# Part of a row-maximum kernel's work moved from VectorE to GpSimd, with TensorE turning the data there and back

## The chip, the core and the metric

The kernel runs on one core of one Trainium2 chip. The metric is the device time of one execution in microseconds (us). Executions are sorted into fast and slow by their time and by the clock in their records, and experiments are compared with runs of the kernel before that were made on the same chip in the same rounds. "Span" is the profiled time from the first to the last instruction; it is about 2 us shorter than the device time.

## The reference

The input has 32 x 512 rows of 1024 numbers in fp32; the output is the maximum of each row.

```python
"x": np.random.randn(32, 512, 1024).astype(np.float32)
return np.max(x, axis=-1).astype(np.float32)
```

These are 16,384 rows. With one row on each of 128 partitions, they make 128 groups of 128 x 1024 elements. Such a group is called a *block* below: 0.52 MB, of 67.1 MB in all.

## The kernel before

Each load brings several blocks into a ring in SBUF (`ring` in the profile), and one VectorE instruction reduces all of them along the free dimension. The list of load sizes starts large and ends small, so that little is left to reduce once the last load has landed (one block here, 1.2 us).

```python
BLOCKS = [
    [15, 14, 13],
    [11, 9, 8, 7],
    [6, 6, 5, 4, 4, 4, 3, 2],
    [2, 2, 2, 2, 2, 1, 1, 1, 1, 1, 1, 1],
]
RING = 46
...
            xc = ring[:, at:at + g, :]
            nc.sync.dma_start(out=xc, in_=xb[:, b:b + g, :])
            nc.vector.reduce_max(out=res[:, first + b:first + b + g], in_=xc, axis=X)
...
        nc.scalar.dma_start(out=dst, in_=res[:, first:first + S])
```

Of the kernel before, what the change touches and what calls it, by code (L numbers as in the profile page):

```python
# [1 line left out]

# [4 lines left out]


F32 = mybir.dt.float32



BLOCKS = [
    [15, 14, 13],
    [11, 9, 8, 7],
    [6, 6, 5, 4, 4, 4, 3, 2],
    [2, 2, 2, 2, 2, 1, 1, 1, 1, 1, 1, 1],
]
RING = 46


@with_exitstack
def kernel(
    ctx: ExitStack,
    tc: tile.TileContext,
    x: bass.AP,
    out: bass.AP,
):
    nc = tc.nc
    P = 128  # L30
    X = mybir.AxisListType.X

    xf = x.flatten_outer_dims()
    N, D = xf.shape
    I = N // P
    of = out.flatten_outer_dims()

    once = ctx.enter_context(tc.tile_pool(name="once", bufs=1))
    ring = once.tile([P, RING, D], F32)
    res = once.tile([P, I], F32)  # L40

    at = first = 0
    for loads in BLOCKS:
        S = sum(loads)
        xb = xf[first * P:(first + S) * P, :].rearrange("(p i) d -> p i d", p=P)
        b = 0
        for g in loads:
            if at + g > RING:
                at = 0
            xc = ring[:, at:at + g, :]  # L50
            nc.sync.dma_start(out=xc, in_=xb[:, b:b + g, :])  # L51
            nc.vector.reduce_max(out=res[:, first + b:first + b + g], in_=xc, axis=X)  # L52
            at += g
            b += g
        dst = bass.AP(tensor=of.tensor, offset=of.offset + first * P, ap=[[S, P], [1, S]])
        nc.scalar.dma_start(out=dst, in_=res[:, first:first + S])
        first += S
    assert first == I


# [1 line left out]
_INS = ['x']  # L62
_OUTS = [((32, 512), 'float32')]


# [23 lines left out]
```

## Time and profile before

| | kernel before |
|---|---|
| device time, median of 3 runs | 165.6 us (165.55 to 165.71) |
| span | 163.6 us |
| VectorE busy | 138.4 us, 27 instructions |
| VectorE idle, waiting for a load | 22.8 us, of which 21.4 before the first |
| end of the last reduction | 161.25 us |
| last load complete on all 16 DMA engines (trace) | 159.6 us |

Busy time plus idle time gives the end of VectorE: 138.4 + 22.8 = 161.2 us. The lines behind the table are in the prediction.

### The profile page before, as it was taken

The page shows a single profiled execution, that of the slowest core. Times are in us where ns is not written, and L with a number is a line of the kernel's source. Part 1 is how long each engine was busy: PE and PEld are TensorE (multiplying, and loading weights), DVE is VectorE, ACT ScalarE, POOL GpSimd, SP SyncE. Part 2 cuts the span into 40 slices and gives each one's busy share as a digit, 9 for nine tenths or more (in the row PEclk, how much of TensorE's full clock was granted, in tenths as well). Part 3 has the DMA queues.
Part 4 walks back from the last instruction along what each step waited for, and adds up shares of the span by engine and source line. Part 5 has one row for each costly group of instructions (what it writes and reads, how often), then busy time and mean ns, then how long its engine had stood idle before and what let it go on. Part 6 is the DMA issues. An engine that isn't in the chain of part 4 may idle for free.

```text
span 163.6 us, 114 instructions
## 1 busy us (share of the span) xinstructions
DVE 138.4 (85%) x27; POOL 0.2 (0%) x4
## 2 busy tenths in 40 slices
DVE  0000079998999899999999999999999999999994
POOL 0000000000000000000000000000000000000000
DMA  7999699999999989999989999999999999999980
GB/s 240 481 481 436 285 449 449 449 449 417 417 417 417 529 353 529 388 425 401 459 385 465 449 401 427 439 400 459 419 421 421 445 405 421 421 421 415 409 339 2
DMA packets 4464, 67.18 MB, mean 411 GB/s; under 512 B 1008, under 2 KB 1008, under 8 KB 1904
## 3 DMA queue, kind: packets, MB, share of 16 engines
q1 hardware_dynamic: 3888, 67.11, 96.3%
q10 hardware_dynamic: 576, 0.07, 0.3%
HBM read 67.11 MB, written 0.07 MB: 411 GB/s over the span
## 4 chain that ended last, share of the span: by engine, by line
DVE 74%; DMA 23%; DVEq 1%; another core or an unknown queue 0%; SPq 0%; issue 0%
DVE res L52 74%; DMA ring<-in_x_dram 23%; DVEq L84 1%; SPq L51 0%
## 5 line engine op out<-in xcount | busy, mean ns | idle before, releaser
L52 DVE TENSOR_REDUCE res<-ring 128x1 f32<-128x1024 f32 (+12 forms) x27 | 138.4, 5205 | 22.8 <-DMA ring<-in_x_dram 22.8
L73 POOL MEMSET const-bfloat16-1.0<- 128x1 bf16 x1 | 0.1, 102 | 0.0
L73 POOL MEMSET const-uint8-127<- 128x1 uint8 x1 | 0.1, 102 | 0.0
L73 POOL MEMSET const-float32-0.0<- 128x1 f32 x1 | 0.1, 99 | 0.2 <-issue 0.2
L73 POOL MEMSET const-float32-1.0<- 128x1 f32 x1 | 0.1, 99 | 0.0
## 6 DMA issues: line engine op xcount, KB each, us to landing
ring<-in_x_dram SPq DMA_DIRECT2D x1, 7680.0 KB, 20.6
ring<-in_x_dram SPq DMA_DIRECT2D x1, 7168.0 KB, 37.2
ring<-in_x_dram SPq DMA_DIRECT2D x1, 6656.0 KB, 52.4
ring<-in_x_dram SPq DMA_DIRECT2D x2, 3072.0 KB, 33.3
ring<-in_x_dram SPq DMA_DIRECT2D x3, 2048.0 KB, 33.8
ring<-in_x_dram SPq DMA_DIRECT2D x6, 1024.0 KB, 23.9
ring<-in_x_dram SPq DMA_DIRECT2D x1, 5632.0 KB, 29.8
ring<-in_x_dram SPq DMA_DIRECT2D x1, 4608.0 KB, 24.9
```

The lines of the kernel that those rows point to most:

```text
L52: nc.vector.reduce_max(out=res[:, first + b:first + b + g], in_=xc, axis=X)
L73: nc = _bacc.Bacc("TRN2", target_bir_lowering=False, num_devices=1)
L84: with _tile.TileContext(nc) as tc:
```

## The change

Its intent is to relieve VectorE. From each of the first nine loads, one or two blocks are kept from it. TensorE turns (transposes) such a block in eight pieces of 128x128, by a product with an identity matrix; ScalarE copies the result from PSUM (`ps` in the profile) to SBUF (`sb`); GpSimd takes the maximum over partitions (an all-reduce); TensorE turns the resulting row back in eight pieces, and VectorE merges eight values a row. That is 14 of 128 blocks, about one row in seven of the large loads. The ring shrinks from 46 to 42 blocks, and the load sizes change.

```diff
 BLOCKS = [
-    [15, 14, 13],
-    [11, 9, 8, 7],
-    [6, 6, 5, 4, 4, 4, 3, 2],
-    [2, 2, 2, 2, 2, 1, 1, 1, 1, 1, 1, 1],
+    [(14, 2), (14, 2), (14, 2)],
+    [(14, 2), (13, 2), (9, 1)],
+    [(7, 1), (8, 1), (6, 1), (5, 0), (3, 0), (3, 0), (2, 0)],
+    [(2, 0), (2, 0), (2, 0), (2, 0), (1, 0), ... eight of these ...],
 ]
-RING = 46
+RING = 42
...
+    make_identity(nc, ident)
...
+        back = psmall.tile([P, m, C], F32)
+        for k in range(m):
+            ps = psum.tile([P, D], F32)
+            for c in range(C):
+                nc.tensor.transpose(out=ps[:, c * P:(c + 1) * P],
+                    in_=rows[:, k, c * P:(c + 1) * P], identity=ident)
...
+            nc.scalar.copy(out=sb, in_=ps)
...
+            nc.gpsimd.partition_all_reduce(top, sb, P, bass_isa.ReduceOp.max)
+            run(backs)
+            ... turn_back, put off in `backs`: eight transposes of top[0:1, ...] into back ...
+        return lambda: nc.vector.reduce_max(out=cols, in_=back, axis=X)
...
+            nc.vector.reduce_max(out=cols[:, :n - m], in_=xc[:, :n - m, :], axis=X)
+            run(late)              # the merge of the load before
+            if m:
+                late.append(merge)
```

More of the change, by code (lines that the diff above doesn't have):

```diff
@@ L6 @@
 from concourse._compat import with_exitstack
+from concourse import bass_isa
+from concourse.masks import make_identity
 F32 = mybir.dt.float32
 BLOCKS = [
-    [15, 14, 13],
-    [11, 9, 8, 7],
-    [6, 6, 5, 4, 4, 4, 3, 2],
-    [2, 2, 2, 2, 2, 1, 1, 1, 1, 1, 1, 1],
+    [(14, 2), (14, 2), (14, 2)],
+    [(14, 2), (13, 2), (9, 1)],
+    [(7, 1), (8, 1), (6, 1), (5, 0), (3, 0), (3, 0), (2, 0)],
+    [(2, 0), (2, 0), (2, 0), (2, 0), (1, 0), (1, 0), (1, 0), (1, 0), (1, 0), (1, 0), (1, 0), (1, 0)],
 ]
-RING = 46
+RING = 42
 @with_exitstack
@@ L34 @@
     N, D = xf.shape
+    C = D // P
     I = N // P
@@ L38 @@
     once = ctx.enter_context(tc.tile_pool(name="once", bufs=1))
+    turn = ctx.enter_context(tc.tile_pool(name="turn", bufs=2))
+    allr = ctx.enter_context(tc.tile_pool(name="allr", bufs=2))
+    psum = ctx.enter_context(tc.tile_pool(name="psum", bufs=3, space=bass.MemoryType.PSUM))
+    psmall = ctx.enter_context(tc.tile_pool(name="psmall", bufs=2, space=bass.MemoryType.PSUM))
     ring = once.tile([P, RING, D], F32)
     res = once.tile([P, I], F32)
+    ident = once.tile([P, P], F32)
+    make_identity(nc, ident)
@@ new lines, with by_gpsimd, turn_back @@
+    backs = []
+    late = []
+    def by_gpsimd(rows, cols, m):
+        back = psmall.tile([P, m, C], F32)
+        for k in range(m):
+            ps = psum.tile([P, D], F32)
+            for c in range(C):
+                nc.tensor.transpose(
+                    out=ps[:, c * P:(c + 1) * P],
+                    in_=rows[:, k, c * P:(c + 1) * P],
+                    identity=ident,
+                )
+            sb = turn.tile([P, D], F32)
+            nc.scalar.copy(out=sb, in_=ps)
+            top = allr.tile([P, D], F32)
+            nc.gpsimd.partition_all_reduce(top, sb, P, bass_isa.ReduceOp.max)
+            run(backs)
+            def turn_back(top=top, k=k):
+                for c in range(C):
+                    nc.tensor.transpose(
+                        out=back[:, k, c:c + 1],
+                        in_=top[0:1, c * P:(c + 1) * P],
+                        identity=ident[0:1, 0:1],
+                    )
+            backs.append(turn_back)
+        return lambda: nc.vector.reduce_max(out=cols, in_=back, axis=X)
@@ L42, with run @@
+    def run(calls):
+        while calls:
+            calls.pop(0)()
     at = first = 0
     for loads in BLOCKS:
-        S = sum(loads)
+        S = sum(n for n, m in loads)
         xb = xf[first * P:(first + S) * P, :].rearrange("(p i) d -> p i d", p=P)
         b = 0
-        for g in loads:
-            if at + g > RING:
+        for n, m in loads:
+            if at + n > RING:
                 at = 0
-            xc = ring[:, at:at + g, :]
-            nc.sync.dma_start(out=xc, in_=xb[:, b:b + g, :])
-            nc.vector.reduce_max(out=res[:, first + b:first + b + g], in_=xc, axis=X)
-            at += g
-            b += g
@@ L55 @@
-        dst = bass.AP(tensor=of.tensor, offset=of.offset + first * P, ap=[[S, P], [1, S]])
-        nc.scalar.dma_start(out=dst, in_=res[:, first:first + S])
+            xc = ring[:, at:at + n, :]
+            nc.sync.dma_start(out=xc, in_=xb[:, b:b + n, :])
+            cols = res[:, first + b:first + b + n]
+            if m:
+                merge = by_gpsimd(xc[:, n - m:, :], cols[:, n - m:], m)
+            else:
+                run(backs)
+            nc.vector.reduce_max(out=cols[:, :n - m], in_=xc[:, :n - m, :], axis=X)
@@ L57, with store @@
+            run(late)
+            if m:
+                late.append(merge)
+            at += n
+            b += n
+        def store(first=first, S=S):
+            dst = bass.AP(tensor=of.tensor, offset=of.offset + first * P, ap=[[S, P], [1, S]])
+            nc.scalar.dma_start(out=dst, in_=res[:, first:first + S])
+        late.append(store)
         first += S
+    run(late)
     assert first == I
```

## The prediction

Its sum came to this: outside the all-reduces 4.6 us a group, an estimate for the transposes, the copy, the turns back, the hand-overs, the merge (0.17 us, estimated from the 0.15 us an instruction and 1.066 us a block of the trace before); nine groups 41.4; the last merge at 20.2 + 112.0 + 41.4 = 173.6; the end of VectorE at 173.6 + 33.3 = 206.9; and with the tail and the offset 211 us, stated as 210.

> **What bounds the kernel now.** I read the page from the top: the busy times, the 40 slices, the DMA queues, the chain that ended last. Then I asked for the groups by shape, and for stretches of the span.
>
> ```profile
> span 163.6 us, 114 instructions
> DVE 138.4 (85%) x27; POOL 0.2 (0%) x4
> DVE  0000079998999899999999999999999999999994
> DMA  7999699999999989999989999999999999999980
> q1 hardware_dynamic: 3888, 67.11, 96.3%
> DVE 74%; DMA 23%; DVEq 1%; another core or an unknown queue 0%; SPq 0%; issue 0%
> ```
>
> VectorE (DVE) is busy for 85% of the span, and the load queue holds the 16 DMA engines for 96.3%: two resources close to full. GpSimd (POOL) does nothing, and TensorE and ScalarE have no row. The chain names VectorE for 74%, but it only follows the engine that finished last; it does not say that a faster VectorE would end sooner. For that I compare the two rates.
>
> ```profile
> L52 DVE TENSOR_REDUCE res<-ring 128x15 f32<-128x15360 f32 x1 | 16.2, 16153 | 21.4 <-DMA ring<-in_x_dram 21.4
> L52 DVE TENSOR_REDUCE res<-ring 128x14 f32<-128x14336 f32 x1 | 15.1, 15087 | 0.8 <-DMA ring<-in_x_dram 0.8
> L52 DVE TENSOR_REDUCE res<-ring 128x13 f32<-128x13312 f32 x1 | 14.0, 14020 | 0.6 <-DMA ring<-in_x_dram 0.6
> L52 DVE TENSOR_REDUCE res<-ring 128x2 f32<-128x2048 f32 x6 | 13.2, 2282 | 0.0
> ...
> L52 DVE TENSOR_REDUCE res<-ring 128x1 f32<-128x1024 f32 x7 | 8.0, 1216 | 0.0
> ```
>
> I call 1024 columns of all 128 partitions a block; there are 128 blocks. Two blocks take 2282 ns and one 1216, so VectorE needs 1.066 us a block and 0.15 us an instruction. The third load started VectorE at 54.06 us and the second at 38.33 (the chain in order of time), so 13 blocks came in 15.73 us: 1.21 us a block. **Transfers are the slower of the two.** All 128 blocks cost 128 x 1.21 = 154.9 us plus some 3 us to start. VectorE catches up with them through ever smaller loads:
>
> ```profile
> 158.00:160.00 2.00, 2.00 (x2) 0.00 (x0) 1.00 0.42 168
> 160.00:162.00 2.00, 1.25 (x2) 0.00 (x0) 1.00 0.00 0
> 162.00:164.00 2.00, 0.00 (x0) 0.00 (x0) 1.00 0.05 4
> ```
>
> The columns are the stretch, its length, VectorE busy, POOL busy, clock, DMA share, GB/s. Loads fill 0.42 of the stretch from 158 on, so their bytes end near 158.8 us. The last reduction starts at 160.0 and ends at 161.25. At most 1.2 us of VectorE backlog can be taken away; the rest of the end is one reduction and a store of 2.35 us. That is the ceiling of the gain: 0.7%.
>
> [...]
>
> **The change part by part.** Removed from VectorE: 14 of 128 blocks, two from each of five loads and one from each of four, 14 x 1.066 = 14.9 us. Added to it: nine tiny merges over 8 or 16 elements, about 0.17 us each, 1.5 us. By busy time alone VectorE would drop to about 125 us.
>
> Added elsewhere: 112 full transposes (14 x 8), 14 copies PSUM to SBUF on ScalarE, 14 all-reduces on GpSimd, 112 small turns back. Only the all-reduces are long. I have no duration for one, so I estimate from the change itself. It gives GpSimd two blocks in a 14-block load, which takes 14 x 1.21 = 16.9 us to arrive: whoever sized this believed in at most 8.4 us each. If sized against VectorE alone, six blocks to one, it is 6 x 1.066 = 6.4. I take **8 us**, near the top, as the transfer rate is the one to keep up with.
>
> Now the order, which the diff does not show. The source puts the merge of a load after VectorE's reduction of the next load, and a turn back after the next transposes, to hide GpSimd. I compared the compiled order of both kernels engine by engine, and **the scheduler undoes that**. VectorE is to run: reduce load 0, merge load 0, reduce load 1, merge load 1, and so on through nine merges; only then the last 16 reductions, of 29 blocks. TensorE is to run: transposes of load 0, its turns back, transposes of load 1. The engines keep this order. So the transposes of a load wait for the previous all-reduces, and VectorE cannot start a load before the previous merge. Nine groups become one serial chain.
>
> One group costs, outside the all-reduces: [...] merge 0.17; [...] Sum 4.6. The second transposes and copy lie beside the first all-reduce, and VectorE's own 12 blocks (12.9 us) beside the two. A two-block group takes 2 x 8 + 4.6 = 20.6 us against an arrival every 16.9; a one-block group 12.6 against 7.3 to 10.9. The chain falls behind from the first load and never recovers.
>
> The sum: the first load, now 14 blocks, lands 1.21 us earlier than the 15 of before, 21.4 - 1.2 = 20.2. Fourteen all-reduces 112.0; nine overheads 41.4. Last merge: 173.6 us. The reductions kept behind it: 5 blocks 5.48, two of 3 6.70, five of 2 11.4, eight of 1 9.7, together 33.3. End of VectorE 206.9, plus the same tail of 2.35: span 209.3, and 2.0 between span and device time as before (165.6 - 163.6): **about 211 us**. I state 210, as a first group or two may overlap better than this.
>
> The ring of 42 instead of 46 blocks holds three loads of 14. A freed slot waits for VectorE and TensorE, so late groups also delay loads. In my reckoning the last loads land near 170 us, long before VectorE reaches them near 205, so this costs nothing more.
>
> **The rivals.** First, **the overlap works**: all-reduces keep up, transfers stay the bound. Then VectorE has no backlog, and the time is 164 to 165.5 us. For it: the proportions look chosen for that, and GpSimd's total, 112 us, fits in the span. Against: the compiled order, and the last large load. Even undelayed, the ninth load cannot land before about 123 us (99 blocks x 1.21, plus 3); one all-reduce of 8 plus 4.6 brings its merge to 135.6, and 33.3 us of reductions behind it end at 169, with tail and offset 173. To stay within 2% (168.9 us), that merge must come by about 131, so the all-reduce must take under 4 us. Second, **a faster all-reduce**, 6.4 us: groups of two need 17.4 us, almost what arrives, the one-block groups still fall behind, and I get 180 to 190. [...]
>
> **Range and chances.** Each microsecond on the all-reduce moves the time by 14, each half microsecond on the overhead of a group by 4.5. From 6.4 us (some 187) to 9 us (some 225), with room for the overhead: 187 to 228. Faster by over 2% is beyond the ceiling of 0.7%, so only a misreading of the transfer limit gives it: 0.02. Within 2% needs all-reduces near 4 us: 0.05. Slower: 0.93.
>
> **What would show it.** In the changed profile, start-to-start times of consecutive GpSimd all-reduces within one load give their cost; I expect 8 us, and some 4.5 us more from the last of one load to the first of the next. VectorE should be idle ahead of its nine merges, waiting for TensorE, by some 7 us for the first loads (20.6 less 12.9 and the merge) and more later, and then run the final 16 reductions without a gap. Loads should stall: mean rate near 67.1 MB / 209 us = 320 GB/s. A VectorE reduction of 12 blocks should still take 12.9 us. The prediction is wrong if idle time before the merges is near zero, if all-reduces are far from 8 us, or if the engines ran in another order than the compiled one.

## The result, and the profile after

| | before | after |
|---|---|---|
| device time, median of 4 runs | 165.57 us | 168.56 us (168.48 to 168.65) |
| span | 163.6 us | 166.8 us |
| VectorE busy | 138.4 us | 124.5 us |
| VectorE idle before a reduction or a merge | 22.8 us | 37.9 + 1.8 us |
| end of the last reduction | 161.25 us | 164.16 us |
| last load complete (trace) | 159.6 us | 160.6 us |

The ratio is 1.0176, with a 95% interval from 1.0161 to 1.0192. A ratio here is the mean time of one kernel's fast runs over that of the other's of the same rounds, so it is not quite the ratio of the medians. The change is, clear of noise, 3.0 us slower. It was predicted at 210.

The page of the changed kernel, first its head, slices and queues, then three of its groups:

```profile
span 166.8 us, 634 instructions
PE 39.7 (24%) x224; PEld 35.3 (21%) x224; DVE 124.5 (75%) x34; ACT 15.5 (9%) x15; POOL 45.8 (27%) x20
DVE  0000099918992899279938999996899599999993
POOL 0000019301940094009501944243163400000000
q1 hardware_dynamic: 3600, 67.11, 94.5%
q8 instruction: 1, 0.02, 0.0%
...
L104 DVE TENSOR_REDUCE res<-ring 128x1 f32<-128x1024 f32 (+8 forms) x25 | 124.0, 5009 | 37.9 <-DMA ring<-in_x_dram 37.9
L71 POOL PARTITION_ALL_REDUCE top<-sb x14 | 45.1, 3254 | 74.4 <-ACT sb L69 74.4
...
L83 DVE TENSOR_REDUCE res<-back 128x2 f32<-128x16 f32 (+1 forms) x9 | 1.5, 163 | 1.8 <-PE back L76 1.8
```

An all-reduce takes 3.25 us, not 8, and is still the longest of the steps added (eight transposes in a row take 1.97 us, a copy 1.01, eight turns back 1.01); the fourteen keep GpSimd busy for 45.1 us, not 112. VectorE does work 13.9 us less (138.4 - 124.5), as forecast. But its slices have holes in the first half, where before there were 8s and 9s once it had started, and its idle time went from 22.8 to 39.7 us. The account closes: 161.25 - 13.9 + 16.9 = 164.25, against a measured end of 164.16. **All the relief became waiting, and 3 us more.** VectorE's timeline shows where (start, duration, engine, line, operation; the idle time before it in brackets):

```profile
54.90 12.95 DVE L104 TENSOR_REDUCE res<-ring 128x12 f32<-128x12288 f32 x1 [3.92 <-DMA ring<-in_x_dram]
67.77 0.17 DVE L83 TENSOR_REDUCE res<-back 128x2 f32<-128x16 f32 x1
71.88 12.95 DVE L104 TENSOR_REDUCE res<-ring 128x12 f32<-128x12288 f32 x1 [3.95 <-DMA ring<-in_x_dram]
...
132.11 0.17 DVE L83 TENSOR_REDUCE res<-back 128x1 f32<-128x8 f32 x1 [1.82 <-PE back L76]
132.19 31.97 DVE L104 TENSOR_REDUCE res<-ring 128x5 f32<-128x5120 f32 x16
```

In the early loads VectorE finishes its 12 blocks and waits 3.9 us for the next load: work taken from it here only lengthens that wait. At the ninth load it waits 1.82 us for the merge, and behind that merge come 29 blocks without one pause to the end. A wait of VectorE there is paid in full. The group that makes it wait:

```profile
124.63 1.97 PE L63 MATMUL ps<-ident,ring 128*128 128x128 f32 x8
126.69 1.01 ACT L69 COPY sb<-ps 128x1024 f32<-128x1024 f32 x1 [6.37 <-PE ps L63]
127.79 3.22 POOL L71 PARTITION_ALL_REDUCE top<-sb  x1 [4.16 <-ACT sb L69]
131.07 1.01 PE L76 MATMUL back<-ident,top 1*128 1x1 f32 x8 [4.47 <-POOL top L71]
```

From turning to merge it takes 7.5 us, while VectorE's share of that load, 5 blocks, takes 5.48.

The clock that TensorE was granted is 0.50 in this stretch and 1.00 in the first groups. That is no cause of note: from the first transpose to the copy it takes 2.06 us here and 1.98 us in the first group, and the four runs of e_onelib below, at mean clocks from 0.604 to 1.0, lie between 168.50 and 168.61 us.

Two questions were left. Is the prediction's chain right and only one duration wrong? And what made up the 3 us: besides the wait of 1.8 us, the loads themselves come about 1 us later to the end.

### The profile page after: what moved, and what is told of

Read it like the earlier page. It is cut to its first block, busy times and chain, and to the rows that moved or that the text cites. A ratio compares the mean times of both kernels' runs of the same rounds, so it can differ in the third digit from the quotient of the medians.

```text
span 166.8 us, 634 instructions
## 1 busy us (share of the span) xinstructions
PE 39.7 (24%) x224; PEld 35.3 (21%) x224; DVE 124.5 (75%) x34; ACT 15.5 (9%) x15; POOL 45.8 (27%) x20
## 4 chain that ended last, share of the span: by engine, by line
DMA 55%; DVE 33%; issue 3%; POOLq 2%; POOL 2%; PE 2%; DVEq 1%; ACT 1%; SPq 0%; ACTq 0%
DMA ring<-in_x_dram 55%; DVE res L104 33%; POOLq L144 2%; POOL top L71 2%; PE ps L63 1%; DVEq L144 1%; ACT sb L69 1%; PE back L76 1%; SPq L98 0%; DVE res L83 0%; ACTq L69 0%
## 5 line engine op out<-in xcount | busy, mean ns | idle before, releaser
L104 DVE TENSOR_REDUCE res<-ring 128x1 f32<-128x1024 f32 (+8 forms) x25 | 124.0, 5009 | 37.9 <-DMA ring<-in_x_dram 37.9
L71 POOL PARTITION_ALL_REDUCE top<-sb x14 | 45.1, 3254 | 74.4 <-ACT sb L69 74.4
L63 PE MATMUL ps<-ident,ring 128*128 128x128 f32 x112 | 25.7, 419 | 49.2 <-DMA ring<-in_x_dram 49.2
L63 PEld LDWEIGHTS ps<-ident,ring 128*128 128x128 f32 x112 | 22.4, 224 | 49.6 <-issue 43.4
L69 ACT COPY sb<-ps 128x1024 f32<-128x1024 f32 x14 | 14.2, 1012 | 111.5 <-PE ps L63 111.5
L76 PE MATMUL back<-ident,top 1*128 1x1 f32 x112 | 14.1, 243 | 43.2 <-POOL top L71 43.2
L76 PEld LDWEIGHTS back<-ident,top 1*128 1x128 f32 x112 | 12.9, 214 | 47.0 <-POOL top L71 47.0
L83 DVE TENSOR_REDUCE res<-back 128x2 f32<-128x16 f32 (+1 forms) x9 | 1.5, 163 | 1.8 <-PE back L76 1.8
## 6 DMA issues: line engine op xcount, KB each, us to landing
ring<-in_x_dram SPq DMA_DIRECT2D x1, 4096.0 KB, 17.2
```

Source lines behind the costliest of these rows:

```text
L63: nc.tensor.transpose(out=ps[:, c * P:(c + 1) * P], in_=rows[:, k, c * P:(c + 1) * P], identity=ident,)
L69: nc.scalar.copy(out=sb, in_=ps)
L71: nc.gpsimd.partition_all_reduce(top, sb, P, bass_isa.ReduceOp.max)
L76: nc.tensor.transpose(out=back[:, k, c:c + 1], in_=top[0:1, c * P:(c + 1) * P], identity=ident[0:1, 0:1],)
L83: return lambda: nc.vector.reduce_max(out=cols, in_=back, axis=X)
L104: nc.vector.reduce_max(out=cols[:, :n - m], in_=xc[:, :n - m, :], axis=X)
```

## The experiments

Twelve runs, all correct. "Last load" is the time at which the last of the 16 DMA engines finished its share of the last load, from the trace; "VectorE end" is the end of the last reduction in the profile.

| run | device time, median | ratio to before (95%) | last load | VectorE end |
|---|---|---|---|---|
| before (all rounds) | 165.5 to 165.6 | 1 | 159.6 | 161.25 |
| after | 168.56 | 1.0176 (1.0161 to 1.0192) | 160.6 | 164.16 |
| e_double | 188.1 | 1.1355 (1.1333 to 1.1377) | 173.9 | 183.7 |
| e_order | 167.26 | 1.0097 (1.0083 to 1.0111) | 161.0 | 163.1 |
| e_vector | 169.40 | 1.0228 (1.0214 to 1.0242) | 160.4 | 165.3 |
| e_lib | 165.38 | 0.9985 (0.9971 to 0.9998) | 159.9 | 161.6 |
| e_ident | 165.53 | 0.9999 (0.9985 to 1.0012) | 159.9 | 161.6 |
| e_onelib | 168.56 | 1.0181 (1.0166 to 1.0195) | 160.6 | 164.2 |
| e_best0 | 167.01 | 1.0089 (1.0074 to 1.0104) | 160.8 | 162.8 |
| e_best | 167.24 | 1.0101 (1.0086 to 1.0117) | 160.7 | 163.0 |
| e_fetch | 166.52 | 1.0064 (1.0052 to 1.0076) | 160.9 | 162.6 |
| e_nofetch | 166.00 | 1.0027 (1.0010 to 1.0045) | 159.7 | 161.35 |
| e_short | 166.84 | 1.0067 (1.0044 to 1.0090) | 160.8 | 162.9 |
| e_short2 | 166.10 | 1.0020 (0.9997 to 1.0044) | 159.7 | 160.9 |

### e_double: every all-reduce done twice

```diff
-            nc.gpsimd.partition_all_reduce(top, sb, P, bass_isa.ReduceOp.max)
+            nc.gpsimd.partition_all_reduce(once_more, sb, P, bass_isa.ReduceOp.max)
+            nc.gpsimd.partition_all_reduce(top, once_more, P, bass_isa.ReduceOp.max)
```

> Each of the 14 all-reduces is done twice (3.2 us more each, result unchanged). Theory A (the prediction's chain is right in kind, only its duration of one all-reduce was too long): two-block groups then take 2 x 6.45 + 4.3 = 17.2 us against an arrival every 17.0, one-block groups 10.7 against 7.3 to 10.9, so the groups fall behind and all of the 29 blocks behind the last merge are pushed out: device time 187 us, from 184 to 190. Rival B (GpSimd is idle for nearly three quarters of the span, so its time hides in that slack): under 172 us.

188.1 us. VectorE's timeline, then two of GpSimd's lines:

```profile
39.01 12.94 DVE L107 TENSOR_REDUCE res<-ring 128x12 f32<-128x12288 f32 x1
56.32 0.17 DVE L86 TENSOR_REDUCE res<-back 128x2 f32<-128x16 f32 x1 [4.38 <-PE back L79]
56.41 12.94 DVE L107 TENSOR_REDUCE res<-ring 128x12 f32<-128x12288 f32 x1
...
151.63 0.17 DVE L86 TENSOR_REDUCE res<-back 128x1 f32<-128x8 f32 x1 [5.21 <-PE back L79]
```

```profile
24.61 3.25 POOL L73 PARTITION_ALL_REDUCE once_more<-sb  x1 [13.33 <-ACT sb L70]
27.96 3.22 POOL L74 PARTITION_ALL_REDUCE top<-once_more  x1
```

Now VectorE waits for the merge in each group, the reduction of the next load starts right behind it, and the last merge comes at 151.6 instead of 132.1. Merges of two-block groups follow each other after 17.4 us (17.2 expected), those of one-block groups after 10.8 (10.7). That is the chain of the prediction. Its own remark for all-reduces of 6.4 us, "some 187", is met within about 1 us. The rival, that GpSimd's time hides in its slack, is out by 16 us.

### e_order: VectorE held to the order of the source

```diff
-        return lambda: nc.vector.reduce_max(out=cols, in_=back, axis=X)
+        return lambda: tc.keep_in_program_order(nc.vector.reduce_max(out=cols, in_=back, axis=X))
```

The same was done for the other reduction. Each merge then follows the reduction of the next load.

> The changed kernel, with VectorE held to the order of the source, so that each merge comes after the next load's reduction. Theory A (the 1.8 us in which VectorE waits for the ninth merge is pushed to the end, because VectorE has 29 blocks behind it and no slack): the wait goes and the device time falls by 1.7 us, to 166.8. Rival B (VectorE's lateness at the end comes from the late landings alone, and the wait would be taken up by idle time further on): no change, 168.5.

167.26, 1.3 us less than the changed kernel where 1.7 were expected. The wait for the merge is gone:

```profile
125.21 5.48 DVE L104 TENSOR_REDUCE res<-ring 128x5 f32<-128x5120 f32 x1
130.60 0.15 DVE L83 TENSOR_REDUCE res<-back 128x1 f32<-128x8 f32 x1
131.04 5.49 DVE L104 TENSOR_REDUCE res<-ring 128x5 f32<-128x5120 f32 x1 [0.28 <-DMA ring<-in_x_dram]
136.44 0.15 DVE L83 TENSOR_REDUCE res<-back 128x1 f32<-128x8 f32 x1
136.51 26.58 DVE L104 TENSOR_REDUCE res<-ring 128x3 f32<-128x3072 f32 x15
```

VectorE starts the tenth load as it lands, at 131.04, instead of at 132.19, and ends at 163.1, one microsecond earlier. In this profile the loads came 0.5 us later still than in the changed kernel (161.0 at the end), which accounts for most of what is missing. So the order costs about half of the 3 us.

### e_vector: the new load sizes and ring alone

The kernel before with the load sizes and ring of the change, every block on VectorE.

> The kernel before with the load sizes and the ring of 42 of the changed kernel, all blocks on VectorE: no GpSimd, TensorE or ScalarE work. If the sizes are chosen for the shared work and are bad without it, VectorE, which has about 138.2 us of work, idles 20.2 us before the first load and about 1.9 us before each of three more, ends near 164.2 us and the device time is 168.5 us: as slow as the change. If the sizes cost nothing, 165.6. The first load of 14 blocks should land at 20.2 us, not 21.0 as in the changed kernel, if something GpSimd brings with it delays the loads.

169.40: the new sizes, with the smaller ring, cost 3.8 us, somewhat more than expected; no run tells the two apart. They are right only if VectorE is relieved. Within these sizes the detour over GpSimd is worth some 0.8 us (169.40 against 168.56; by the ratios 1.0228 against 1.0176); it does not pay for the sizes. The first load of 14 blocks started VectorE at 20.49 here, against 21.03 in the changed kernel, so something in the change delays even the first load. The last load of e_vector is complete only at 160.4, though its trace has no instruction packet (see below): its last two loads are spread over 1.4 us from the first engine to the last, those before them over 0.9. Why is not shown; VectorE, which ends at 165.3, was not waiting for them.

### e_lib and e_ident: what GpSimd brings, one part at a time

Added to the kernel before: in e_lib one tiny all-reduce, in e_ident the building of the identity; neither result is used.

```diff
+    nc.gpsimd.partition_all_reduce(tiny[:, 1:2], tiny[:, 0:1], P, bass_isa.ReduceOp.max)   # e_lib
+    make_identity(nc, ident)                                                              # e_ident
```

> The kernel before with one all-reduce of 128x1 elements added at the start, its result unused. Theory A [...]: the first load lands 0.9 us later than 21.4, at 22.3, and everything stays late: 166.3 to 166.6 us against 165.6. Rival B (the late first landing of the changed kernel comes from its sizes or from other engines): no change within 0.2 us.

> The kernel before with only the building of the 128x128 identity added (a memset and an affine select on GpSimd, result unused). The added all-reduce alone changed nothing (e_lib). Theory A (the affine select, which waited 10.3 us in the changed kernel[...]): the affine select waits about 10 us here too, the first load lands 0.8 to 1.8 us later than 21.4, and the device time is 166.4 to 167.4. Rival B (the lateness comes from ScalarE's table load or from TensorE's and ScalarE's own instructions): 165.6, first landing 21.4.

Theory A failed in both: 165.38 and 165.53, no slower than before. The affine select ran at 1.01 us without a wait, and the first loads landed at 21.7, within 0.4 of before (21.39). Neither operation alone delays the first load by more than 0.4 us, or the device time at all.

### e_onelib: both operations, the all-reduce first

```diff
-    make_identity(nc, ident)
+    first_use = nc.gpsimd.partition_all_reduce(tiny[:, 1:2], tiny[:, 0:1], P, bass_isa.ReduceOp.max)
+    with tc.issue_after(first_use.ins):
+        make_identity(nc, ident)
```

In the changed kernel the affine select starts at 11.26 us, after 10.33 us in which it waited for nothing that the profile shows; in e_ident, where it is alone, it started at 1.01. Here a tiny all-reduce is put ahead of it.

> The changed kernel with one tiny all-reduce ahead of the building of the identity[...]. Theory A: the affine select starts in the first 2 us instead of at 11.3, the first load of 14 lands at 20.3 to 20.5 instead of 21.0, and the device time falls by 0.6 to 0.9 us, to 167.6 to 168.0. Rival B (lateness from elsewhere): 168.5.

The start went as theory A said. These are the affine select and the first reduction, first of the changed kernel:

```profile
11.26 0.28 POOL masks.py:199 TENSOR_SCALAR_AFFINE_SELECT ident<-ident 128x128 f32<-128x128 f32 x1 [10.33 <-issue]
21.03 12.95 DVE L104 TENSOR_REDUCE res<-ring 128x12 f32<-128x12288 f32 x1 [21.03 <-DMA ring<-in_x_dram]
```

and of e_onelib:

```profile
1.55 0.29 POOL masks.py:199 TENSOR_SCALAR_AFFINE_SELECT ident<-ident 128x128 f32<-128x128 f32 x1
20.36 12.95 DVE L108 TENSOR_REDUCE res<-ring 128x12 f32<-128x12288 f32 x1 [20.36 <-DMA ring<-in_x_dram]
```

The time did not move: 168.56 again. The trace, which records when each DMA engine finished its share of a load, tells why. In the changed kernel 12 engines had finished the first load by 20.12 us and four only at 20.76 to 21.01. In e_onelib all 16 had finished by 20.34. But its last load was complete on 15 engines at 159.57 and on the sixteenth at 160.56. Both kernels have a packet of 16 KB on the instruction queue (the row "q8 instruction" of the page) at 76.2 us, which took 0.96 to 0.97 us. VectorE starts a load when the slowest engine has finished it (20.36 after 20.34), and here no late engine made up for its delay: in e_onelib one engine finished the fifth load at 88.0, 15 by 87.0, and that 1 us is still there at the end. The first lateness was removed, a second one set the same end.

The start divides all profiles cleanly: in the five kernels with this repair (e_onelib, e_best0, e_best, e_short, e_short2) the first load was complete at 20.3 to 20.5, in the three without it (the changed kernel, e_order, e_double) at 21.0 to 21.8. ScalarE's table load, which three of the five have at 0.73 to 0.74 us like the three without the repair (0.72), is thus no cause.

### e_fetch and e_nofetch: a longer program, and nothing else

```diff
+    for _ in range(224):      # 96 in e_nofetch
+        nc.tensor.transpose(out=unread, in_=tiny[0:1, :], identity=tiny[0:1, 0:1])
```

These tiny turns lie at the start of the kernel before, and nobody reads their result.

> The kernel before with 224 tiny TensorE turns added at the start (as many as the changed kernel has in all), their result unread. Theory A ([...]a 16 KB packet of the instruction queue holds one of the 16 DMA engines for 1 us, and that engine's share of every later load stays 1 us late): the row of the instruction queue appears, the last load lands near 160.6 instead of 159.6, and as VectorE had 0.5 us in hand there the time rises by about 0.5 us, to 166.0 to 166.4. Rival B (the late landings come from the block sizes or from GpSimd): 165.6, last landing 159.6.

> Control of e_fetch: the same with 96 tiny turns. Theory A: [...]no instruction packet appears, time 165.6, last landing 159.6 to 159.9. If TensorE's work itself delays loads: as e_fetch or part of it.

e_fetch is 0.64% slower: 166.52, a little over the 166.0 to 166.4 that were expected, as the first packet (at 13.95 us) already holds up the first load. Its queues on the page, and its first reduction:

```profile
q1 hardware_dynamic: 3888, 67.11, 95.5%
q10 hardware_dynamic: 576, 0.07, 0.3%
q8 instruction: 2, 0.03, 0.1%
...
22.68 16.15 DVE L58 TENSOR_REDUCE res<-ring 128x15 f32<-128x15360 f32 x1 [22.68 <-DMA ring<-in_x_dram]
```

The first load starts VectorE at 22.68 instead of 21.39, with 15 engines done at 21.38 and one at 22.66; the last load is complete at 160.9 instead of 159.6. The instruction packets took 0.88 and 0.91 us. VectorE's 138.4 us of work simply start 1.3 us later. The control was expected to have no packet; it had one, but after its loads (at 164.9). It landed its last load at 159.7 in the profile, and cost 0.27%. Its six times run from 165.5 to 166.46, but their spans only from 163.7 to 164.1, where the kernel before has 163.6 to 164.2 in the same rounds; e_fetch has 164.7 to 165.0. So the control's excess lies outside the span and does not point to late loads; what it is, is not shown.

### e_best0, e_best, e_short, e_short2: can the idea be repaired?

e_best0 joins the two repairs (e_order and e_onelib). e_best also gives GpSimd one block of the tenth load.

> Both repairs in the changed kernel: source order on VectorE, and the tiny all-reduce ahead of the identity. If the two causes are independent they add: 168.5 less 1.5 less 0.8, so 166.0 to 166.4 us. If the late landings were hidden behind VectorE: as e_order, 167.3.

> As e_best0, with one block of the tenth load (of 5) given to GpSimd too. VectorE then has 1.07 us less behind the tenth landing and comes close to the landing of the last load, the bound that is left: 165.2 to 165.7 us, so even with the kernel before or 0.2% faster. If the tenth group's merge arrives too late and VectorE waits for it: 166.3 or more.

e_best0, at 167.01, missed its 166.0 to 166.4: the start is repaired, but the instruction packet at 76.3 us leaves the last load at 160.8, so it is level with e_order within the intervals. e_best, at 167.24, failed in the way its last sentence foresaw: VectorE waits 1.14 us for the tenth merge:

```profile
139.59 0.17 DVE L87 TENSOR_REDUCE res<-back 128x1 f32<-128x8 f32 x1 [1.14 <-PE back L80]
```

e_short then leaves the first four loads wholly to VectorE (6 GpSimd blocks instead of 14), and e_short2 adds one block of the tenth load with its merge two loads later.

```diff
-    [(14, 2), (14, 2), (14, 2)],
-    [(14, 2), (13, 2), (9, 1)],
+    [(14, 0), (14, 0), (14, 0)],
+    [(14, 0), (13, 2), (9, 1)],
```

> Both repairs, and no GpSimd block in the first four loads, where VectorE waits for the load anyway: 6 GpSimd blocks instead of 14, 192 TensorE instructions instead of 448. Theory A: no instruction packet, last landing 159.6; VectorE starts the tenth load as it lands near 129.7 and needs 32.05 us from there: end 161.8, device time 165.8 to 166.1. If the first eight GpSimd blocks were worth something: 167 or more.

> As e_short, with one block of the tenth load given to GpSimd and its merge placed two loads later. VectorE has 1.07 us less to do at the end and should finish near 161.0, one reduction behind the last landing: 165.1 to 165.5 us, level with the kernel before or up to 0.3% faster. If its merge is waited for, or an instruction packet appears (224 TensorE instructions): 166 or more.

e_short, at 166.84, was forecast at 165.8 to 166.1: its trace still has an instruction packet, at 127 us, and its last load was complete at 160.8. Still, with eight GpSimd blocks fewer it is no slower than e_best0: **those eight blocks were worth nothing**, as VectorE waits for the tenth load in both (first e_best0, then e_short):

```profile
130.77 5.49 DVE L108 TENSOR_REDUCE res<-ring 128x5 f32<-128x5120 f32 x1 [0.29 <-DMA ring<-in_x_dram]
...
130.87 5.49 DVE L108 TENSOR_REDUCE res<-ring 128x5 f32<-128x5120 f32 x1 [1.53 <-DMA ring<-in_x_dram]
```

In e_short2's profile the packet came after the last load (complete at 159.7; 8 GB/s, or about 16 KB, were moved between 162 and 164 us), VectorE ended at 160.9, before the kernel before, and the span was 163.5. Its timed runs fall into two kinds, 165.15 and 165.30, as forecast, against 166.05 to 166.34 (spans 163.4 and 163.5 against 164.2 to 164.5). That an earlier packet makes the second kind is likely but not shown, as one run alone is profiled. The median of 166.10 misses the forecast and is not better than before. No version of the change here beats the kernel before.

## Why the prediction was wrong

**What bounds the kernel now: right.** Transfers are slower than VectorE (1.21 against 1.066 us a block), and the ceiling of the gain is under 1%. No version ended earlier than that ceiling. It was itself put too high: 1.2 us was read from a DMA share averaged over 2 us, while the trace has the last load complete at 159.56, and so only 0.5 us before the last reduction starts.

**The step that failed: "I take 8 us".** The term "Fourteen all-reduces 112.0" measured 14 x 3.22 = 45.1 us, and one all-reduce was half of even the 6.4 us at the low end of the range. The value was inferred from the shares of work in the change, on the belief that its author had filled GpSimd; in fact two all-reduces take 6.4 us of the 16.9 that a load takes to arrive. The step after it fell with it: "A two-block group takes 2 x 8 + 4.6 = 20.6 us against an arrival every 16.9" became 10.7 against 16.9, so the chain keeps up with the large loads and stalls only at the ninth.

**The overhead of a group: right in its sum.** Forecast 4.6, an estimate; measured 7.5 - 3.2 = 4.3 us in the group shown, 4.4 with the merge. The terms measured: 1.97 us for eight fp32 transposes in a row, 246 ns each; 1.01 us for a copy; 1.01 us for eight turns back; 0.3 us in all for the four hand-overs.

**The order and the serial chain: right in kind.** VectorE ran in the compiled order: the merge at 67.77 us comes before the next load's reduction at 71.88. e_double brings the chain back, at 188.1; its late groups delay loads too, as the prediction said (the last is complete at 173.9, not 160.6). In the changed kernel the issue of loads waited 87.2 us in all for VectorE's reductions, 13.0 for a merge and 0.2 for the transposes. And e_order shows that the compiled order costs about 1.3 us even at 3.2 us an all-reduce. The prediction also gave the condition for staying within 2%, 168.9 us: an all-reduce under 4 us. It was 3.2, and the time was 168.56. That this fits so closely is partly luck: in its own sum the merge had to come by about 131 and came at 132.1, as the ninth load landed at 124.4 instead of 123; but the reductions behind it took 32.0 us, not 33.3.

**VectorE's work: right.** About 125 us were forecast and 124.5 measured, and a reduction of 12 blocks took 12.95 us beside GpSimd's work, as 1.066 x 12 + 0.15 = 12.94 gives; one of 5 blocks took 5.48 us, with an all-reduce beside it (at 127.79) and in the kernel before. The rival that GpSimd's work slows VectorE is out for these reductions.

**The first load at 20.2: wrong by 0.8 us,** of which 0.3 are there without GpSimd too (20.49 in e_vector). The prediction counted only the data of the loads and did not speak of single DMA engines. In the changed kernel, where the affine select waited 10.33 us, four engines finished the first load 0.6 to 0.9 us after the other twelve; in e_fetch, whose program is longer by 224 turns, one engine finished it 1.3 us after the other fifteen, with an instruction packet of 0.9 us before.

Of the 2.9 us by which VectorE ends later, about 1.6 are the wait for the ninth merge (132.19 against 130.54, where the tenth load had landed) and about 0.9 are the late loads (130.54 against 129.62 in e_short2, whose loads were not late). The rest of about 0.3 is put down to the new sizes, which no run shows by itself. The first is shown by e_order, less its own later loads. That loads stay late to the end after an instruction packet is shown by e_fetch (160.9 against 159.6). That four engines are late at the start in the changed kernel, and none with the tiny all-reduce ahead of the affine select, is shown by the repair (21.01 against 20.34). What holds the four is not shown; no packet of another queue is in the trace there.

## What to carry to other kernels

Ask where the relieved engine waits: here, work taken from it ahead of a wait for a transfer was worth nothing, and work that came back to it late, with a long row of instructions behind, cost its whole wait. An estimate of an operation inferred from how somebody has balanced a kernel is an upper bound at best, not a value; give it a range that reaches far below. And where transfers fill the DMA engines to 96%, count what else rides on them: the slowest of the 16 set every landing here. Packets of 0.9 to 1.0 us on the instruction queue left single engines 1.0 to 1.3 us late to the end of the loads, and e_fetch was 0.64% slower.
